# Hybrid encoder layer on one core: router in written order with early indices, first token statistics by pairs, last epsilon on GpSimd

## The chip, the cores and the metric

One core of one Trainium2 chip runs the whole layer in one launch. The metric is the device time of that launch in microseconds (us). Engines are called as in the profile: PE (TensorE matmul), PEld (its weight loads), DVE (VectorE), ACT (ScalarE), POOL (GpSimd), SP (the DMA queue that SyncE issues). Each engine runs its own instructions in the order in which they stand in the program, and waits on semaphores for what others make.

## The reference, cut

```python
# x: (1, 1024, 1024) float32, one layer, h = x at first
n = rms_norm(h, norm1)                    # per token, eps 1e-6
proj = n @ W_in                           # 6656 columns, in blocks
# GDN: 8 heads of 128, both directions, gated delta rule in chunks of 64
# SSD: 16 heads of 64 in 2 groups, both directions, Mamba-2 scan in chunks of 64;
#      decay masks exp(where(incl, cs_i - cs_j, -inf))
h = h + concat(o_gdn, y_ssd) @ W_out
n2 = rms_norm(h, norm2)
aff = softmax(n2 @ W_router)              # 16 experts
vals, idx = top_k(aff.T, 128)             # each expert takes its 128 best tokens
xs = n2[idx]
y = (silu(xs @ W_gate) * (xs @ W_up)) @ W_down * vals
out = rms_norm(h + scatter_add(y, idx), norm_f)
```

## The kernel before, in words

Tokens lie 8 tiles of 128 deep (`x_107` to `x_114`), and 1024 features are 8 blocks `d`. Float32 products are made of rounded parts: an operand is split into a high part (ACT copies it to fp32r: `whi`, or `n`) and the rest (DVE subtracts: `wlo`), and PE multiplies high by high, high by low and low by high. A step of the program is a small function that is put on a list with a slot by `at()` (L134). `flush(name)` (L137) then runs them: for the mixer in the order of a table of 3602 numbers, packed as text in `ORDER["mixer"]`, where a number is the list's index of the step (a step that yields stands several times); for the experts by a heap over the slots.

**Start.** `x_sq(t)` (L344) squares and sums a token tile on ACT, `x_stat(h)` (L347) makes the inverse norm of four tiles at a time (a DVE add-multiply, then the power on POOL through `rsqrt`, L199), `x_scale(t)` (L353) scales a tile on DVE, and `x_turn(h, d)` (L356) transposes four tiles on PE (L359) and evicts them as the two parts `n` (ACT, then DVE). PE turns the small weights `rows` at L334 ahead of that. `w_half` (L250) then does a first projection by halves, L471 turns its result, and `rates` exponentiates a small table of decay rates (`Rf<-Rf 128x48`, on ACT), which it loads from DRAM.

**Mixer.** `w_load`, `w_split` (`whi` on ACT, `wlo` on DVE) and `w_unit` (L242, 6 matmuls) make the projections of 128 columns at a time; convolutions, GDN heads and SSD heads run beside them. For an SSD head, POOL makes a decay mask `E` (a subtraction in L123 and a select, L560), ACT takes its exponential (`E<-E`), DVE goes on. Then the output projection (L1289) adds blocks into `n` with DVE, and `open_moe` (L1445) makes constants on POOL, among them `digit` (L1473, 45 small instructions). All this is inside `tc.manual_schedule()` (L1482): it goes out as it is written.

**Router** (L1485 to 1570). This part is outside of manual scheduling; the tile scheduler places it. Softmax of the logits `lg`; then a search for the 128th largest value of each expert in 15 rounds (L1527 to 1539): DVE compares (`msk`), PE counts with 8 small matmuls (L1533), DVE picks (`best`, a reduction, `trial`). The first expert's weights are split meanwhile: ACT copies the high parts, and DVE makes 12 half rests (`rest()`, `place<-place 128x512`), which are written at one per round from round 2 on. After the search, `ge`, `need`, `sel` and `posx` give every token's place in its expert's list.

**Experts.** `rt(e)` (L1573) makes one-hot tiles `oh` from `posx` (8 DVE instructions), sums them against `aux` on PE (L1580), builds the index `idx` and the gate value on DVE, and issues the gather of 128 token rows (`place<-n2D,idx`, POOL, L1591). `xt` transposes them on PE (L1612) and `gm`, `gs`, `gu`, `ht`, `dm`, `ys` are the expert's products (L1648, L1664, L1667). Expert weights come through SP (`e_load`), 30 of them ahead of the router, each later one when a tile is given back. At the end `TAIL` (L1759) writes out the last norm: `f_sq` (ACT square and sum), `f_st` (L1743: DVE adds epsilon, POOL takes the power), `f_mul` or `f_sc`, `f_out`.

Of the kernel before, what the change touches and what calls it, by code (L numbers as in the profile page):

```python
# [43 lines left out]
        "c-l>v1FU9EvxU35tGlY-v2EM7ZQHhO+qP}nwr$(it@HlLmzyVR)#}x?_nyflXELLdQQ=i2<&;)Y6)CH{3a40wQn3_>;;9%yY!zCCQDIdC6-UKY"  # L44
        "5mjUrP^hA-#G*vviB)_RMN%S_OGQ%&RdSU>6ko_Gq*4ilgerH?Q>Z*Duga%Vs?;h;kQORUkn}=Y*-Ed9sB)6hs&ql}tE56vQ8J;Js-rT<%%BR0"
        "G71GnnN@L>No7$BRJI`5h4MmHRY+A(g;fc;%_LiyRY_G!l~!f`qvHSbGOCiQEM7%b6|W|$rD_NJ>Z*pMnyRzpW~!d5FSD$wE0k58R2T98(IDsz"
        "|2vme6I55#O?6j2R8JKO8cEYwHBr4(Q%TK*R;s1ytNN&Zs<mpPdaG%wtu#|qe>FgSq8g|MsljT93JvX4d(}Zrl8qTcXy~Yhso`pbx-O?O5Dvma"
        "1PB9RVW^5I9tk4DR5enKQlr%vHCaW0v1*)}suDpohz@gAbeO4*L0Pz>W~*6hj*1HDAsu9Z7!Xs)2$>)j#D+K!7iO!uDjsBp_>ce+LKe88ZmFy="
        "UR@P(LJ}wk*HjKsE|{n0tIaAKY*q_ZQb-DkVUe1ywy4CA401zq$OF?=dH5|&3P=fgAs^(20+0$)!(z2W{Zu#AFCjZr5Gui6RSEtn1xwX3wOs8~"
        "D^x*PsVYK6NCRo1FsxFQVYOPL0M@E?YO7kWHmHq4P57g#KoxNf$7LReLQn(@REACJkV3cwyOjk8JJfEqN9|Jw)G64j_N$_BP@RS|a28HLF*pf_"  # L50
        ")nRo+*rtxELHZ<|gF0|r9aAUNNp(t{hYN5KPOIWj0!qReRZ6r=U54$dD%60>@EXpk^YUvstFFOyxB=DSg1V%t!7I1|SK$q86|W9&;T^n(4{%Xk"
        "R#((bxCQs%wh97w)E#wK-BWkqBYc8;sut9Sx=;`93wKq0xUcT32I38&5j=tisuPqJzYAZXF*Jck>XCY=9;>F%3?9Q{Nl&0TJW(y+DYS%E@K8Nb"
        "t)UG(fT!xIdI-<dGx7HDT!ruqy1)zdLcJ0?!b|l!NLxwI;f;DLsU38e^iFk$cd8d`gC5Wm-l{(EUWM=iKB#S?x2iY9(Cy)q>I!|KAH-CjRDb9X"
        "1BBu5Sq&C_R0H9o>I{S6i~1s`4$^giZ|XA)fuS<H!7vyBUm%PQqra=~Y6MJxZ}3%(g3<6py_ED-eTOkH62`(fm?+&3B@Wwx;3tfi?Mad*!F2c~"
        "@;a0brvsY73%_9p{DBz|keiv}Ghmjm19n0<9YN2A+0sVVb6^haf(UxID722KC&Ltoq$BG9MA7qL4@A{b^<Ic3IlBG_O7DaD!c=*BKMdCMVH(U8"
# [53 lines left out]
def trunk(ctx, tc, x, norm1_w, w_in, conv_w, conv_b, gdn_A_log, gdn_dt_bias, gdn_norm_w,  # L109
# [1724 lines left out]
```

## Time and profile before

| | before |
|---|---|
| three timed runs, us | 1672.53, 1676.93, 1685.21 (median 1676.93) |
| the profiled execution, us | 1671.89 |
| its span, us | 1670.2 |
| mean granted PE clock | 0.972 |
| busy us: PE, PEld | 1550.8 (93%), 1264.7 (76%) |
| busy us: DVE, ACT, POOL | 1211.5 (73%), 982.0 (59%), 730.0 (44%) |
| DMA | 254.20 MB, mean 152 GB/s |

Times in rows count from the span's start. Busy time is the time in which an engine ran an instruction; an idle stretch stands in brackets at the instruction that ended it, with what released it. The granted clock is the share of full speed that PE was given: 1.00 is 2.4 GHz and 0.50 is 1.2 GHz.

### The profile page before, as it was taken

What the parts mean: (1) busy time and instruction counts of PE and PEld (TensorE: products, weight loads), DVE (VectorE), ACT (ScalarE), POOL (GpSimd) and SP (SyncE); (2) the same over time, 40 slices, a digit from 0 to 9 for tenths busy, and PEclk for the clock granted to TensorE, in tenths of its full rate; (3) what the DMA queues carried; (4) which work ended last, traced back from release to release, by engine and by line L of the source; (5) the groups of instructions that cost most, each with busy time, mean ns of one, the idle gap of its engine ahead of it and who ended that gap; (6) DMA issues with size and microseconds to landing.
All of it is one profiled execution on the core that took longest, in us unless ns stands there. A gap on an engine that the chain in (4) does not pass through costs nothing. (4 is left out here: it accounts for less than half of the span.)

```text
span 1670.2 us, 23559 instructions
## 1 busy us (share of the span) xinstructions
PE 1550.8 (93%) x8290; PEld 1264.7 (76%) x8290; DVE 1211.5 (73%) x2045; ACT 982.0 (59%) x1788; POOL 730.0 (44%) x533
## 2 busy tenths in 40 slices
PE   5989999999999999998989999998996499899997
PEld 4768888888889888887765687687885377677774
DVE  4686768686767677757779976864556598789875
ACT  5476485858586767465542574243455177677764
POOL 1285263647454654425898877713032011111112
PEclk9999999999999999999999999999997599999999
DMA  4322223223231322222332245457787289999955
GB/s 137 98 60 43 45 65 68 75 56 87 42 98 28 105 70 63 39 70 95 108 101 70 67 135 172 150 183 263 256 284 291 111 311 372 329 382 375 389 184 213
DMA packets 174784, 254.20 MB, mean 152 GB/s; under 512 B 54370, under 2 KB 112027, under 8 KB 174667
## 3 DMA queue, kind: packets, MB, share of 16 engines
q1 hardware_dynamic: 170202, 236.45, 42.3%
q0 software_dynamic: 4464, 16.25, 3.8%
q8 instruction: 65, 1.06, 0.3%
q14 instruction: 53, 0.43, 0.1%
HBM read 221.01 MB, written 31.65 MB: 151 GB/s over the span
## 5 line engine op out<-in xcount | busy, mean ns | idle before, releaser
L242 PE MATMUL pj<-n,whi 128*128 128x512 f32 x1664 | 482.5, 412 | 9.8 <-ACT whi L129 7.5
L242 PEld LDWEIGHTS pj<-n,whi 128*128 128x128 f32 x1664 | 301.0, 190 | 79.2 <-ACT whi L129 11.1
L242 PE MATMUL pj<-n,wlo 128*128 128x512 f32 x832 | 263.4, 398 | 3.6 <-DVE wlo L123 3.5
L123 DVE TENSOR_TENSOR place<-place 128x1024 fp32r<-128x1024 f32 (+1 forms) x182 | 208.0, 1184 | 27.8 <-ACT place L129 27.8
L126 DVE SCALAR_TENSOR_TENSOR cacc<-pj,cols,cacc 128x1023 f32<-128x1023 f32 (+2 forms) x156 | 199.3, 1278 | 22.8 <-POOL cacc L123 20.1
L123 POOL TENSOR_TENSOR cacc<-cacc,cpr 128x1021 f32<-128x1021 f32 x60 | 145.7, 2429 | 153.4 <-ACT cacc L129 81.0
L1648 PE MATMUL pj<-place 128*128 128x512 f32 x768 | 198.3, 410 | 2.0 <-DVE place L123 1.3
L129 ACT ACTIVATE place<-place 128x1024 fp32r<-128x1024 f32 (+1 forms) x181 | 181.5, 1053 | 16.8 <-issue 8.5
L242 PEld LDWEIGHTS pj<-n,wlo 128*128 128x128 f32 x832 | 156.2, 189 | 45.8 <-DVE wlo L123 8.3
L1648 PEld LDWEIGHTS pj<-place 128*128 128x128 f32 x768 | 144.5, 192 | 40.6 <-DVE place L123 5.3
L123 DVE TENSOR_TENSOR n<-n 128x1024 fp32r<-128x1024 f32 x64 | 84.3, 1327 | 68.9 <-ACT n L129 40.7
L1591 POOL DMA_INDIRECT place<-n2D,idx x16 | 17.4, 1088 | 259.4 <-ACT place L129 93.7
L129 ACT ACTIVATE n<-n 128x1024 fp32r<-128x1024 f32 x64 | 66.7, 1056 | 104.1 <-DMA n<-in_w_out_dram 55.2
L123 DVE TENSOR_TENSOR wlo<-wraw,whi 128x512 fp32r<-128x512 f32 x106 | 96.7, 914 | 15.0 <-ACT whi L129 14.9
L1289 PE MATMUL pj<-n 128*128 128x512 f32 x384 | 97.4, 408 | 4.1 <-DVE n L123 4.1
L129 ACT ACTIVATE whi<-wraw 128x512 fp32r<-128x512 f32 x106 | 65.8, 625 | 57.7 <-PE pj L242 47.5
L129 ACT ACTIVATE place<-g 128x512 fp32r<-128x512 f32 (+1 forms) x48 | 26.9, 561 | 110.4 <-PE g L1612 106.2
L1289 PEld LDWEIGHTS pj<-n 128*128 128x128 f32 x384 | 72.5, 191 | 24.2 <-DVE n L123 5.8
L129 ACT ACTIVATE cpr<-pj,cols 128x1021 f32<-128x1021 f32 x60 | 66.5, 1109 | 26.6 <-PE pj L242 16.9
L129 ACT ACTIVATE u<-c,bt 128x128 f32<-128x128 f32 x128 | 39.6, 363 | 60.1 <-DVE ud L123 58.4
L123 POOL TENSOR_TENSOR ex<-N,nm 128x512 f32<-128x512 f32 x48 | 62.2, 1304 | 14.6 <-PE g L785 9.9
L123 DVE TENSOR_TENSOR E<-E,tb_dt 128x1024 f32<-128x1024 f32 x32 | 56.9, 1790 | 15.5 <-ACT E L129 15.3
(328 smaller groups left out, 3202.9 us busy)
## 6 DMA issues: line engine op xcount, KB each, us to landing
place<-in_w_gate_dram SPq DMA_DIRECT2D x64, 512.0 KB, 9.3
place<-in_w_up_dram SPq DMA_DIRECT2D x64, 512.0 KB, 8.7
place<-in_w_down_dram SPq DMA_DIRECT2D x64, 512.0 KB, 9.8
wraw<-in_w_in_dram SPq DMA_DIRECT2D x106, 256.0 KB, 3.3
E<-rowsD SPq DMA_DIRECT2D x32, 512.0 KB, 3.8
n<-mixD SPq DMA_DIRECT2D x64, 256.0 KB, 3.4
n<-in_w_out_dram SPq DMA_DIRECT2D x64, 256.0 KB, 4.4
dec<-rowsD SPq DMA_DIRECT2D x16, 512.0 KB, 7.7
```

What stands on the lines that cost most here:

```text
L123: eng.tensor_tensor(o, a, b, op=op)
L126: V.scalar_tensor_tensor(o, a, s, b, op0=op0, op1=op1, **kw)
L129: S.activation(o, i, f, **kw)
L242: T.matmul(pj[c0][:, hs], lhsT=w[:, d % 4, :], rhs=nn[d][:, hs], start=(d == 0 and a == 0), stop=(d == ND - 1 and a == 2))
L1289: T.matmul(wst["po", r][t], lhsT=m[:, 0, ts], rhs=w[:, 1, :], start=(k == k0 and a == 0), stop=(k == k1 - 1 and a == 2))
L1591: nc.gpsimd.indirect_dma_start(out=ex["xs", e], out_offset=None, in_=n2D[:, :], in_offset=ex["idx", e])
L1648: T.matmul(po, lhsT=xT[:, j, d % 4, :], rhs=wt[k][:, HALF[dd]], start=(d == 0 and a == 0), stop=(d == ND - 1 and a == 2))
```

## The change

Five edits:

1. The statistics of token tiles 0 to 3 are made as soon as two tiles are summed (columns 0:2, then 2:4), and tiles 0 and 1 are scaled ahead of the second pair; tiles 4 to 7 as before.
2. `ORDER["mixer"]` is a new permutation of the same steps (3602 numbers before and after).
3. The router stands inside `tc.manual_schedule()` and so goes out as written; the two casts and two subtractions that fill `aux` move into rounds 0 and 1, and a half rest stands in each of rounds 2 to 13.
4. `rt` no longer gathers; `gx(e)` does. `rt(0)` to `rt(3)` all stand ahead of the first expert, with a yield of 0.5 instead of 6.0, and `gx` stands where the gather stood, 8.7 slots into an expert, from expert 2 on.
5. `f_st` adds epsilon on POOL instead of DVE.

```diff
 ORDER = {
     "mixer":
-        "c-l>v1FU9EvxU35tGlY-v2EM7ZQHhO+qP}nwr$(it@HlLmzyVR)#}x?_nyflXELLdQQ=i2<&;)Y6)CH{3a40wQn3_>;;9%yY!zCCQDIdC6-UKY"
+        "c-lRe1CX@65`}|KI+@S5ZQHhO+qP}nwr$(CZCm&3)L*xrI*rqvytBJCyR$-QVTBjrgc3$L5lX}Y@kD45UW65KL?jVGL=`bWY!OjJ7A&L)BLad%"
...
     def x_sq(t):
         act(junk1, xt[t], AF.Square, accum_out=ss1[:, t:t + 1])
+        if t == 3:
+            scale(0)
+            scale(1)
+        if t in (1, 3):
+            stat(slice(t - 1, t + 1))
+
+    def stat(hs):
+        V.tensor_scalar(ss1[:, hs], ss1[:, hs], 1.0 / D, EPS, op0=OP.mult, op1=OP.add)
+        rsqrt(rstd[:, hs], ss1[:, hs])

     def x_stat(h):
-        hs = slice(h * 4, h * 4 + 4)
-        V.tensor_scalar(ss1[:, hs], ss1[:, hs], 1.0 / D, EPS, op0=OP.mult, op1=OP.add)
         yield 0.1
-        rsqrt(rstd[:, hs], ss1[:, hs])
+        if h:
+            stat(slice(4, NT))

     def x_scale(t):
+        if t > 1:
+            scale(t)
+
+    def scale(t):
         V.tensor_scalar(xt[t], xt[t], rstd[:, t:t + 1], None, op0=OP.mult)
...
-    act(lg, lg, AF.Exp)
-    act(warm, mhalf[:, :1], AF.Silu)
...
+    with tc.manual_schedule():
+        act(lg, lg, AF.Exp)
+        act(warm, mhalf[:, :1], AF.Silu)
...
+        V.memset(best[0][:, 0, :], 0.0)
+        V.tensor_copy(trial, over3(tv["digit"][:, 0, :]))
+        res = hp.tile(SE, F32, name="res")
+        for j in range(15):
+            tt(V, msk3, aff[:, :, None, :].to_broadcast(S4), trialf[:, None].to_broadcast(S4), OP.is_ge)
+            if j < 2:
+                src = res if j else aff
+                V.tensor_copy(aux[:, :, :, 2 + j], src)
+                tt(V, aux[:, :, :, 4] if j else res, src, aux[:, :, :, 2 + j], OP.subtract)
+            elif halves:
+                rest(*halves.popleft())
...
-        yield 6.0
+        yield 0.5 if e < 4 else 6.0
...
-        yield 0.2
+        ex["idx", e], ex["val", e] = bass.IndirectOffsetOnAxis(ap=idx[:, :1], axis=0), ax[:, 6:7]
+
+    def gx(e):
         ex["xs", e] = take()
-        ex["idx", e], ex["val", e] = bass.IndirectOffsetOnAxis(ap=idx[:, :1], axis=0), ax[:, 6:7]
         nc.gpsimd.indirect_dma_start(out=ex["xs", e], out_offset=None, in_=n2D[:, :], in_offset=ex["idx", e])
...
     def f_st(t):
-        V.tensor_scalar(ssf[:, t:t + 1], ssf[:, t:t + 1], D * EPS, None, op0=OP.add)
+        P.tensor_scalar(ssf[:, t:t + 1], ssf[:, t:t + 1], D * EPS, None, op0=OP.add)
...
-    at(-30, rt, 0)
-    at(-29, rt, 1)
+    for e in range(4):
+        at(-30 + 1.9 * e, rt, e)
+        if e < 2:
+            at(-28.8 + 1.9 * e, gx, e)
     for e in range(NE + 1):
         b = EP * e
         if e < NE:
             if e + 2 < NE:
-                at(b + 2, rt, e + 2)
+                if e > 1:
+                    at(b + 2, rt, e + 2)
+                at(b + 8.7, gx, e + 2)
```

Counted over the whole program, ACT has 48 table loads instead of 52, DVE has 7 TENSOR_SCALAR fewer (8 of `f_st` gone, one for the split statistics more), and POOL has 8 TENSOR_SCALAR and one power more; everything else has the same count.

At the start, on ACT, the two orders differ as follows; `n<-g,cols` are the evictions of `x_turn`, `Rf<-Rf 128x48` is the exponential in `rates`, `O<-pj` evicts the result of `w_half`, and + is the new order.

```order
 L129 ACTIVATE n<-g,cols 128x512 x9
+L129 ACTIVATE whi<-wraw 128x512
+L129 ACTIVATE O<-pj 128x1024
+L129 ACTIVATE whi<-wraw 128x512
+L129 ACT_TABLE_LOAD
+L129 ACTIVATE tb_beta<-qd 128x128
+L129 ACT_TABLE_LOAD
+L129 ACTIVATE Rf<-Rf 128x384
+L129 ACTIVATE whi<-wraw 128x512
 L129 ACTIVATE Rf<-Rf 128x48
-L129 ACTIVATE whi<-wraw 128x512
-L129 ACTIVATE n<-g,cols 128x512 x2
```

The exponential `Rf<-Rf 128x48` stood ahead of the last two evictions and now stands behind all of them, behind `O` and behind two table loads.

On DVE, in the output projection of the kernel before, two instructions of the router (L1525 and L1526) stand among the mixer's additions `n`:

```order
L1224 TENSOR_SCALAR Y<-Y,ry 128x512 x8
L123 TENSOR_TENSOR n<-n 128x1024 x8
L1525 MEMSET best_11578 128x16
L1526 COPY trial<-digit 128x48
L123 TENSOR_TENSOR n<-pj,n 128x512 x4
L123 TENSOR_TENSOR n<-n 128x1024 x4
```

In the changed kernel the same two stand on DVE in the router, behind the softmax:

```order
L1502 TENSOR_REDUCE den<-lg 128x8
L1503 RECIPROCAL den<-den 128x8
L123 TENSOR_TENSOR aff<-lg,den 128x128
L1538 MEMSET best_11582 128x16
L1539 COPY trial<-digit 128x48
L123 TENSOR_TENSOR msk_11581<-aff,trial 128x384
L1545 CAST aux<-aff 128x128
```

They moved some 50 rows down, from the output projection to just ahead of the first round.

On ACT, at the first decay masks of the SSD heads, the order before has the weight split `whi` (of the projection block at column 5632) behind two exponentials `E`:

```order
L129 ACTIVATE xk<-g 128x4x128 x2
L129 ACT_TABLE_LOAD
L129 ACTIVATE E<-E 128x1024
L129 ACTIVATE xk<-g 128x4x128
L129 ACTIVATE E<-E 128x1024
L129 ACTIVATE whi<-wraw 128x512
L129 ACTIVATE cacc<-pj,cols 128x1024
```

The changed kernel has it in front of them, with the block's second split behind:

```order
L129 ACTIVATE xk<-g 128x4x128 x3
L129 ACTIVATE whi<-wraw 128x512
L129 ACT_TABLE_LOAD
L129 ACTIVATE E<-E 128x1024 x2
L129 ACTIVATE whi<-wraw 128x512
L129 ACTIVATE cacc<-pj,cols 128x1024
L129 ACTIVATE cpr<-pj,cols 128x1021
```

One `whi` moved from behind the two exponentials to ahead of them.

## Rows read from the trace of the kernel before

**Rows 1.** The page's part 1: busy us, share of span, instructions.
```profile
PE 1550.8 (93%) x8290; PEld 1264.7 (76%) x8290; DVE 1211.5 (73%) x2045; ACT 982.0 (59%) x1788; POOL 730.0 (44%) x533
```

**Rows 2.** Waits of PE: who waits, for whom, us in total, times, longest.
```profile
PE c L1533 <- DVE msk L123: 29.1, 15, 4.3
...
PE pj L242 <- ACT whi L129: 7.5, 2, 4.6
...
PE pj L1289 <- DVE n L123: 4.1, 3, 2.7
```

**Rows 3.** Windows: stretch and length; busy PE, PEld, DVE, ACT, POOL; clock; DMA.
```profile
43.60:50.40 6.80, 5.64 (x18) 4.27 (x18) 2.30 (x6) 3.91 (x5) 0.00 (x0) 0.50 0.13 39
784.30:787.70 3.40, 2.85 (x7) 2.28 (x8) 2.88 (x3) 3.38 (x5) 2.92 (x3) 0.50 0.23 58
...
920.00:940.00 20.00, 19.21 (x71) 12.56 (x70) 19.20 (x22) 7.22 (x8) 19.85 (x12) 1.00 0.22 66
1328.00:1640.00 312.00, 299.55 (x1404) 231.55 (x1402) 261.34 (x403) 217.29 (x266) 44.05 (x29) 0.99 0.89 318
```

**Rows 4.** Timeline of the start: start, us, engine, line, operation, [idle before <-releaser].
```profile
13.89 0.45 PE L334 MATMUL g<-ident,rows 128*128 128x128 f32 x1 [5.02 <-DMA rows<-in_conv_b_dram]
...
33.83 0.69 ACT L129 ACTIVATE n<-g,cols 128x512 fp32r<-128x512 f32 x1 [0.46 <-PE g L359]
...
41.05 0.24 ACT L129 ACTIVATE Rf<-Rf 128x48 f32<-128x48 f32 x1 [6.53 <-DMA Rf<-in_ssd_A_log_dram]
...
41.72 1.25 ACT L129 ACTIVATE n<-g,cols 128x512 fp32r<-128x512 f32 x2
...
42.44 0.50 PE L250 MATMUL pj<-n,whi 128*128 128x512 f32 x1 [3.56 <-ACT n L129]
```

**Rows 5.** Timeline of DVE in the output projection.
```profile
1133.90 0.07 DVE L1525 MEMSET best<- 128x16 f32 x1 [0.49 <-ACT zt L129]
1137.50 0.20 DVE L1526 COPY trial<-digit 128x48 int32<-128x48 int32 x1 [3.52 <-POOL digit L1473]
```

**Rows 6.** Timeline of ACT at the first SSD masks.
```profile
783.22 1.06 ACT L129 ACTIVATE E<-E 128x1024 f32<-128x1024 f32 x1 [2.37 <-POOL E L560]
```

**Rows 7.** Timeline of the router, ACT and DVE.
```profile
1277.22 1.28 ACT L129 ACT_TABLE_LOAD   x1
...
1284.04 0.56 DVE L123 TENSOR_TENSOR msk<-aff,trial 128x384 bf16<-128x384 f32 x1
1284.52 0.68 DVE L123 TENSOR_TENSOR place<-place 128x512 fp32r<-128x512 f32 x1
...
1287.41 0.55 DVE L123 TENSOR_TENSOR msk<-aff,trial 128x384 bf16<-128x384 f32 x1
...
1296.05 0.56 DVE L123 TENSOR_TENSOR msk<-aff,trial 128x384 bf16<-128x384 f32 x1
1297.21 0.21 DVE L126 SCALAR_TENSOR_TENSOR best<-c,trial 128x48 f32<-128x48 f32 x1 [0.60 <-PE c L1533]
...
1297.99 0.56 DVE L123 TENSOR_TENSOR msk<-aff,trial 128x384 bf16<-128x384 f32 x1
```

**Rows 8.** Timeline from `posx` to the first expert, DVE, POOL and PE.
```profile
1316.98 2.69 DVE L1576 TENSOR_SCALAR oh<-slots,posx 128x128 bf16<-128x128 bf16 x16
...
1320.83 1.25 POOL L1591 DMA_INDIRECT place<-n2D,idx  x1 [45.66 <-DVE ax L123]
...
1325.39 1.98 PE L1612 MATMUL g<-ident,place 128*128 128x128 f32 x8 [5.46 <-DMA place<-n2D,idx]
```

**Rows 9.** Timeline of the last norm, POOL and DVE.
```profile
1652.01 1.52 POOL L123 TENSOR_TENSOR rf<-ssf,mhalf 128x1 f32<-128x1 f32 x1 [0.56 <-DVE ssf L1744]
...
1661.13 0.54 POOL L123 TENSOR_TENSOR rf<-ssf,mhalf 128x1 f32<-128x1 f32 x1 [1.46 <-DVE ssf L1744]
...
1662.91 0.20 DVE L1744 TENSOR_SCALAR ssf<-ssf 128x1 f32<-128x1 f32 x2
```

**Rows 10.** Line L1473: ns minimum/median/maximum of one, first and last start.
```profile
L1473 POOL TENSOR_SCALAR digit<-tid x45: 198/208/1232, 1136.9 to 1151.9; 128x1 int32<-128x1 f32 x45
```

More of the change, by code (lines that the diff above doesn't have):

```diff
@@ L1485, in trunk @@
     aff, ones_b, before_b, slots, aux, posx, lg = (tv[n] for n in ("aff", "ones_b", "before_b", "slots", "aux", "posx", "lg"))
-    act(lg, lg, AF.Exp)
-    act(warm, mhalf[:, :1], AF.Silu)
-    den = hp.tile([128, NT], F32, name="den")
-    V.tensor_reduce(den, lg, axis=AX.X, op=OP.add)
-    V.reciprocal(den, den)
-    tt(V, aff, lg, den[:, :, None].to_broadcast(SE), OP.mult)
-    mp = pool("mp")
-    ex = {}
-    halves = deque()
-    def split(w, e, i):
-        raw = eraw.pop(epos[w, e, i])
-        if (w, i) in WHOLE:
-            ex["w", w, e, i] = raw,
-            return None
-        hi, lo = take(F32R), take(F32R)
-        ex["w", w, e, i] = hi, lo
-        act(hi, raw, AF.Copy)
-        return raw, hi, lo
@@ L1507, in rest @@
-    def rest(parts, cols, last):
-        raw, hi, lo = parts
-        tt(V, lo[:, cols], raw[:, cols], hi.bitcast(F32)[:, cols], OP.subtract)
-        if last:
-            give(raw)
-    EARLY = [(w, 0, i) for w in range(2) for i in range(3)]
-    for key in EARLY:
-        parts = split(*key)
-        halves.extend((parts, HALF[h], h) for h in range(2))
-    msk3 = hp.tile([128, NT, 3, NE], BF, name="msk3")
-    best = [hp.tile([128, 4, NE], F32, name=f"best{i}") for i in range(2)]
-    trial = hp.tile([128, 3, NE], I32, name="trial")
@@ L1521, in trunk @@
-    S3 = [128, 3, NE]
-    S4 = [128, NT, 3, NE]
-    trialf = trial.bitcast(F32)
-    over3 = lambda a: a[:, :, None].to_broadcast(S3)
-    V.memset(best[0][:, 0, :], 0.0)
-    V.tensor_copy(trial, over3(tv["digit"][:, 0, :]))
-    for j in range(15):
-        tt(V, msk3, aff[:, :, None, :].to_broadcast(S4), trialf[:, None].to_broadcast(S4), OP.is_ge)
-        if j > 1 and halves:
-            rest(*halves.popleft())
-        pc = ctile([128, 3, NE])
-        for t in range(NT):
-            T.matmul(pc.rearrange("p k e -> p (k e)"), lhsT=ones_b, rhs=msk3[:, t].rearrange("p k e -> p (k e)"),
-                     start=(t == 0), stop=(t == NT - 1))
-        stt(best[j % 2][:, 1:4, :], pc, 127.5, trialf, OP.is_ge, OP.mult)
-        thr = best[1 - j % 2][:, 0, :]
-        V.tensor_reduce(thr, best[j % 2].rearrange("p k e -> p e k"), axis=AX.X, op=OP.max)
-        if j < 14:
-            tt(V, trial, thr.bitcast(I32)[:, None, :].to_broadcast(S3), over3(tv["digit"][:, j + 1, :]), OP.bitwise_xor)
@@ L1553, in trunk @@
-    b_gt, b_eq = pb[:, :NT, :NE], pb[:, :NT, NE:]
-    need = hp.tile([128, 2, NE], F32, name="need")
-    V.tensor_scalar(need[:, 0], pb[:, NT, :NE], -1.0, 128.0, op0=OP.mult, op1=OP.add)
-    V.tensor_scalar(need[:, 1], need[:, 0], 512.0, None, op0=OP.add)
-    needb = lambda i: need[:, i, :][:, None, :].to_broadcast(SE)
-    over = hp.tile(SE, F32, name="over")
-    sel = hp.tile(SE, BF, name="sel")
-    tt(V, over, b_eq, needb(0), OP.subtract)
-    stt(sel, over, 0.0, eq, OP.is_lt, OP.mult)
```

207 lines of the change are left out of this document (126 added, 81 removed).

## The prediction

> **What bounds the kernel now.** I read the page first: PE is busy for 93% of the span and no other engine for more than 76% [rows 1]. So the kernel gets shorter only where PE stands idle or runs at half clock, and I went to PE's waits, ranked, to see whom it waits for [rows 2], and then to the timeline around the long ones. The largest is the router's search, 29.1 us in 15 waits for DVE's compare; two waits of 7.5 us together are for a weight split on ACT (`whi`), and the longest for an addition in the output projection is 2.7 us. The windows show the second price of a wait: the granted clock is at 0.50 (1.2 GHz) in the 6.8 us from 43.6 and in the 3.4 us from 784.3, each right behind an idle PE [rows 3]. Matmul work there runs at half speed, so a stretch costs up to half its length beside the wait: at most 3.4 and 1.7 us.
>
> The expert stage, 1328 to 1640, is 299.6 of 312 us PE [rows 3]. DMA is 0.89 busy there, but a load is issued only when a tile is given back, and tiles are given back by the expert's own progress. I therefore let a gain ahead of the experts move the whole stage; the case against that is a rival below.
>
> **The change, part by part.** All terms are against the profiled execution, 1671.9 us with a span of 1670.2.
>
> *Start (edits 1 and 2).* PE has nothing to do from the last `w_half` matmuls until 42.44, an idle time of 3.56 us that ended with the eviction `n` on ACT. That eviction (two, from 41.72) stood behind the small exponential `Rf`, for which ACT waited 6.53 us until its DMA had landed [rows 4]. The order shows the exponential behind all evictions now, and its consumers later still. Evictions come one per 1.15 us (0.69 of ACT and 0.46 of waiting for PE's next transposes, the row at 33.83). So the last two would start at 33.83 + 1.15 = 34.98 and 36.13 and end near 36.8, in place of 41.72 + 1.25 = 42.97: 6.2 us earlier. The half clock behind that wait, 6.8 us long, costs up to 3.4; the pause before L471 is left and may bring part of it back, so I take 0.9. The pairs let the first tiles be scaled earlier, but the transposes of `x` begin behind the last `rows` turn, which waits for its DMA until 13.89 [rows 4]; its load stands behind as many loads of `x` as before. I give the pairs 0.4. The extra DVE and POOL instruction lie in that wait and cost nothing; without that cover they would cost two short instructions. What is late next is PE's own work: the matmuls of `w_half` behind each eviction. Together **−7.5**; bounds −3 (the eviction pace holds, but heads that are latency chains absorb half) and −10 (the whole half clock is gone and the pairs give 1).
>
> *Output projection (2 and 3).* The tile scheduler had drawn the router's MEMSET and COPY into DVE's mixer stream, where the COPY waited 3.52 us for POOL's `digit` [rows 5]. The additions `n` behind it came late, and PE waited 2.7 us [rows 2]. In the new order the two stand in the router, by when `digit` has been ready for over 100 us (the last starts at 1151.9 [rows 10]). PE then also keeps its clock; as the half clock of the 784 stretch shows, that is up to 1.7 us. I take 2.7 + 1.0 = **−3.7** (0 if the loads of `w_out` are late there anyway, −4.4).
>
> *Router (3).* Three rounds held four half rests each and lasted 3.37 us (1284.04 to 1287.41); a round with none lasts 1.94 (1296.05 to 1297.99). One half takes 0.68 and stands where DVE waits 0.60 for PE's count: from 1284.52 it ends at 1285.20, which is 1.16 after its compare, and without one the next step also starts 1.16 after it (1297.21) [rows 7]. So one half per round is hidden, and 3 × (3.37 − 1.94) = 4.3 us go. The twelve halves now end in round 13, still ahead of the first expert's matmuls. The table load of 1.28 us at 1277.22 stands ahead of the softmax's exponential [rows 7]; a switch to Silu had been put early. It goes behind the exponential. The MEMSET and COPY come onto the path: 0.07 + 0.20 [rows 5]. Together −4.3 − 1.28 + 0.27 = **−5.3** (−4 to −6).
>
> *Early indices (4).* Both `rt` together took 2.69 us of one-hots; alone, the first needs 1.35. Index 0 is thus ready some 1.0 us earlier than at 1320.83, and the gather needs 4.6 us from there to PE's transposes at 1325.39. But now four `rt` stand on DVE ahead of the experts. The small steps of both took 1320.83 − 1319.67 = 1.16, 0.6 each [rows 8], so it is 4 × (1.35 + 0.6) = 7.8 us from 1316.98, and PE's eight matmuls for the fourth index stand ahead of the transposes: 1324.8 plus a part of a microsecond, against 1325.39. I take **0**; bounds −1.0 and +1.0. Gathers on POOL come in the same slots of later experts as before.
>
> *Last norm (5).* `f_st` on DVE queued behind `f_mul` (two of them together at 1662.91, behind a multiply of 1.28 us). On POOL it costs about 0.21 (the median of the small `digit` instructions [rows 10]) and 0.54 for the power [rows 9]. Statistics 6 and 7 would then be ready ahead of their multiplies, and the last multiplies close up: about −1.3. Against that, one power lasted 1.52 instead of 0.54, at 1652.01, with DVE in a multiply of the same kind [rows 9]; if powers stretch so here, one of them puts the last multiply 0.6 back, −0.7. The value is **−0.9**, and +1 is the other bound, when two powers in a row stretch. The Trainium skill (GPSIMD Engine Reference, Key points) says that GpSimd shares its SBUF interfaces with VectorE and contends with DVE instructions that have two SBUF inputs. The trace agrees with 1.52 against 0.54 us; by that rule the term would be −0.7, and by the undisturbed row −1.3.
>
> *Rest of the new table (2).* At the first SSD masks ACT waits 2.37 us for POOL's mask before an `E` exponential [rows 6], and the split `whi` behind it keeps PE waiting. Now this split stands ahead of both exponentials. It is one of the two waits of 7.5 us together, the longer of which is 4.6 [rows 2], so it is 2.9; with half of the 3.4 us at half clock, 4.6. But POOL is as busy as 19.85 of 20 us later in the SSD stage [rows 3], and its work isn't less. Where POOL is the bound, a gain of PE is given back at the next mask. Between −4.6 and 0 I take **−2.3**. The other moved steps I take at 0: their instructions are the same, each moved by some 20 places in 3600.
>
> Sum: −7.5 − 3.7 − 5.3 + 0 − 0.9 − 2.3 = **−19.7**, so 1652.2 in the state of the profiled execution. That one lies 5.0 below the median of the runs, 1676.9, so I forecast **1657 us** for the median; its own range is 1652 to 1663.
>
> **The rivals.**
>
> *Upstream gains are given back.* The start ends earlier, but GDN heads are chains that wait for small instructions of ACT and DVE, and the SSD stage for POOL. For it speaks POOL at 19.85 of 20; against it that PE has so few long waits. With the start at −2 and the table's rest at 0: −2 − 3.7 − 5.3 − 0.9 = −11.9, 1665 us. The expert stage could also return the router's part if its DMA (0.89 busy) doesn't move with the start; −14.4 then, 1662.5.
>
> *The new order also removes the second wait for `whi`.* It is 4.6 and half of a 6.8 us stretch like that at 43.6, 8.0 together. With the first in full: −19.7 − 2.3 − 8.0 = −30, 1647 us. For it: the first such split has moved. Against it: two masks of POOL still stand ahead of the second.
>
> *The other side: new waits for `whi` behind `E`.* The new order puts exponentials back to back and the block's second split behind them. Where POOL is late, each such wait costs up to 8.0. Without the first wait's gain the sum is −17.4, so it decides from three waits on (2.2 × 8.0); slower by over 1% takes 4.3 of them. With five it is −17.4 + 40.0 = +22.6, 1699.5 us. For it: POOL has no slack. Against: only two of these occurred in a mixer of 1260 us.
>
> **How the numbers follow.** My forecast 0.48, gains given back 0.27, second wait removed too 0.15, new waits 0.10. The bound of 1%, about what a measurement of this kernel tells from no change, is at 1660.2 and 1693.7. Four fifths of the forecast's cases lie under 1660.2 (0.39) and all of the third's (0.15): faster 0.54. The rest of the forecast (0.09), the given-back cases (0.27) and new waits that only cancel the gain (0.03) are the same: 0.39. Slower 0.07. The range 1646 to 1673 leaves out the new waits and the lowest part of the third case, some 0.18.
>
> **What would show it.** In the profile after: the evictions at the start without a wait for the rates' DMA, and `w_half` ending near 39; no `digit` wait on DVE; 15 rounds of 1.9 to 2.2 us and no table load ahead of the `lg` exponential; transposes of the first expert as far behind `posx` as before; the tail's powers in sequence on POOL. The prediction is wrong if PE's waits in the SSD stage grow, above all for `whi`, or if the expert stage gets longer than it was.

## The result, and the profile after

The changed kernel takes 1656.83 us (median of 4 runs, 1652.63 to 1659.94) against 1677.95 for the kernel before (4 runs, 1672.53 to 1685.21): 0.987 of it, with a 95% interval of 0.9826 to 0.9914. The forecast was 1657 in a range of 1646 to 1673. The profiled execution took 1656.17 us, with a span of 1654.5 against 1670.2, so the two traces differ by 15.7 us where the sum said 19.7. The account below gives a reason for each.

Part 1 of the page after shows that PE did the same work in a shorter span [rows 1]:

```profile
PE 1550.6 (94%) x8290; PEld 1270.1 (77%) x8290; DVE 1213.4 (73%) x2038; ACT 976.9 (59%) x1784; POOL 731.7 (44%) x542
```

PE's waits after (line numbers are 12 to 18 higher from the middle of the program on) answer [rows 2]:

```profile
PE c L1551 <- DVE msk L123: 23.3, 15, 3.2
...
PE c L1180 <- DVE hs L123: 6.1, 2, 5.3
...
PE pj L1301 <- DVE n L123: 2.4, 3, 1.1
```

The search gave up 5.8 us of waiting, the weight split (7.5 us in two waits) has gone from the list, and the output projection's longest such wait is 1.1 instead of 2.7. But a wait of 5.3 us for `hs`, which was not there before, stands near the top. The windows after show where the clock was at 0.50 (1.2 GHz), and the expert stage:

```profile
40.70:44.10 3.40, 2.75 (x11) 2.56 (x12) 1.18 (x3) 2.80 (x4) 0.00 (x0) 0.50 0.35 97
...
829.20:836.00 6.80, 6.80 (x25) 6.03 (x24) 4.72 (x3) 1.58 (x2) 6.65 (x4) 0.50 0.38 118
866.70:873.50 6.80, 5.52 (x11) 3.50 (x12) 6.32 (x6) 5.81 (x6) 6.73 (x4) 0.50 0.12 35
1314.40:1624.40 310.00, 298.14 (x1388) 231.13 (x1388) 257.93 (x379) 216.27 (x264) 43.47 (x29) 0.98 0.89 321
```

The stretch at the start is half as long as before [rows 3], the one at 784 has moved to 795, and two of 6.8 us stand in the first SSD group, where there was one before (from 876.5).

**Start.** The timeline after, ACT, DVE and PE:

```profile
35.45 1.27 ACT L129 ACTIVATE n<-g,cols 128x512 fp32r<-128x512 f32 x2 [1.15 <-PE g L371]
...
37.04 0.17 DVE L449 TENSOR_REDUCE h<-bd 128x2 f32<-128x8 f32 x1 [1.96 <-POOL bd L403]
...
37.95 1.40 DVE L126 SCALAR_TENSOR_TENSOR n<-g,cols,n 128x512 fp32r<-128x512 f32 x2
...
38.75 0.50 PE L250 MATMUL pj<-n,whi 128*128 128x512 f32 x1 [1.26 <-DVE n L126]
...
41.34 1.97 PE L483 MATMUL g<-ident,O 128*128 128x128 f32 x8 [1.16 <-ACT O L129]
...
49.49 0.23 ACT L129 ACTIVATE Rf<-Rf 128x48 f32<-128x48 f32 x1
```

The last two evictions begin at 35.45 and end at 36.7, as worked out (36.8), and the rates' exponential waits for nothing at 49.49. PE's idle time of 3.56 us [rows 4] is 1.26 now. It isn't zero because a new wait took a part of the place: DVE stood 1.96 us for POOL's block masks (`bd`) ahead of its half of the same evictions.

**Router.** ACT and DVE after:

```profile
1269.49 0.31 ACT L129 ACTIVATE lg<-lg 128x128 f32<-128x128 f32 x1
1269.82 1.28 ACT L129 ACT_TABLE_LOAD   x1
...
1274.72 0.56 DVE L123 TENSOR_TENSOR msk<-aff,trial 128x384 bf16<-128x384 f32 x1
1275.19 0.68 DVE L123 TENSOR_TENSOR place<-place 128x512 fp32r<-128x512 f32 x1
1275.87 0.21 DVE L126 SCALAR_TENSOR_TENSOR best<-c,trial 128x48 f32<-128x48 f32 x1
...
1276.65 0.56 DVE L123 TENSOR_TENSOR msk<-aff,trial 128x384 bf16<-128x384 f32 x1
```

The table load stands behind the exponential, and a round with one half rest lasts 1.93 us, as one without did [rows 7].

**First expert.** DVE, POOL and PE after, to be held against [rows 8]:

```profile
1303.37 1.39 DVE L1589 TENSOR_SCALAR oh<-slots,posx 128x128 bf16<-128x128 bf16 x8
...
1306.30 1.23 POOL L1605 DMA_INDIRECT place<-n2D,idx  x1 [38.47 <-DVE oh L1589]
...
1310.54 1.32 PE L1593 MATMUL c<-aux,oh 128*128 128x5 bf16 x8 [0.89 <-DVE oh L1589]
1311.72 1.95 PE L1626 MATMUL g<-ident,place 128*128 128x128 f32 x8
```

The gather is issued 2.9 us behind the end of `posx` (1303.37) instead of 3.9, and PE turns the gathered rows 8.4 us behind that end, as before: the fourth index's matmuls stand in between and PE waits for nothing else.

**Last norm.** POOL and DVE after, [rows 9]:

```profile
1637.24 1.28 DVE L126 SCALAR_TENSOR_TENSOR place<-place,rf 128x1024 f32<-128x1024 f32 x1 [1.04 <-POOL rf L123]
1637.43 1.18 POOL L1758 TENSOR_SCALAR ssf<-ssf 128x1 f32<-128x1 f32 x1 [0.22 <-ACT place L129]
...
1639.24 0.23 POOL L1758 TENSOR_SCALAR ssf<-ssf 128x1 f32<-128x1 f32 x1
1639.30 1.28 DVE L126 SCALAR_TENSOR_TENSOR place<-pj,rf,place 128x1024 f32<-128x1024 f32 x1 [0.77 <-POOL rf L123]
1639.55 0.57 POOL L123 TENSOR_TENSOR rf<-ssf,mhalf 128x1 f32<-128x1 f32 x1
...
1640.40 0.57 POOL L123 TENSOR_TENSOR rf<-ssf,mhalf 128x1 f32<-128x1 f32 x1
...
1649.09 1.28 DVE L126 SCALAR_TENSOR_TENSOR place<-pj,rf,place 128x1024 f32<-128x1024 f32 x1
```

The epsilon takes 0.22 to 0.25 us on POOL (0.21 had been taken), and twice 1.16 to 1.18, each time beside a multiply of DVE such as the one at 1637.24, which takes both its tensors from SBUF (`place<-place`). Beside the multiply at 1639.30, which takes one from PSUM (`pj`), the power takes 0.57 as elsewhere.

**First SSD group.** The chain to the wait of 5.3 us after, ACT, DVE and PE:

```profile
862.91 1.06 ACT L129 ACTIVATE E<-E 128x1024 f32<-128x1024 f32 x1 [3.01 <-POOL E L572]
...
864.52 0.78 DVE L123 TENSOR_TENSOR wlo<-wraw,whi 128x512 fp32r<-128x512 f32 x1 [2.59 <-ACT whi L129]
865.22 2.11 DVE L123 TENSOR_TENSOR E<-E,tb_dt 128x1024 f32<-128x1024 f32 x1
867.25 0.68 DVE L123 TENSOR_TENSOR hs<-c,hs 128x512 f32<-128x512 f32 x1
...
867.98 2.07 PE L1180 MATMUL c<-xw,Bt 128*128 128x512 f32 x2 [5.30 <-DVE hs L123]
```

ACT waited 3.0 us for POOL's mask, the split behind it came late, DVE waited for the split, and `hs`, for which PE waits, stood behind both. PE waits for another name than in the kernel before; at the end of the chain is the same POOL mask.

### The profile page after: what moved, and what is told of

Same layout as the page of the kernel before. It is cut to its first block, busy times and chain, and to the rows that moved or that the text cites. A ratio compares the mean times of both kernels' runs of the same rounds, so it can differ in the third digit from the quotient of the medians.

```text
span 1654.5 us, 23564 instructions
## 1 busy us (share of the span) xinstructions
PE 1550.6 (94%) x8290; PEld 1270.1 (77%) x8290; DVE 1213.4 (73%) x2038; ACT 976.9 (59%) x1784; POOL 731.7 (44%) x542
## 3 DMA queue, kind: packets, MB, share of 16 engines
q8 instruction: 65, 1.06, 0.3%
## 5 line engine op out<-in xcount | busy, mean ns | idle before, releaser
L242 PE MATMUL pj<-n,whi 128*128 128x512 f32 x1664 | 484.7, 413 | 3.0 <-DVE cacc L126 1.3
L242 PEld LDWEIGHTS pj<-n,whi 128*128 128x128 f32 x1664 | 302.1, 191 | 71.6 <-issue 7.3
L242 PE MATMUL pj<-n,wlo 128*128 128x512 f32 x832 | 263.1, 397 | 0.6 <-DVE wlo L123 0.6
L242 PEld LDWEIGHTS pj<-n,wlo 128*128 128x128 f32 x832 | 157.1, 189 | 40.2 <-DVE wlo L123 1.9
L123 DVE TENSOR_TENSOR wlo<-wraw,whi 128x512 fp32r<-128x512 f32 x106 | 101.8, 964 | 26.4 <-ACT whi L129 26.3
L123 POOL TENSOR_TENSOR E<-E,tb_gc 128x1024 f32<-128x1024 f32 x32 | 65.6, 2048 | 9.7 <-DMA E<-rowsD 4.9
## 6 DMA issues: line engine op xcount, KB each, us to landing
place<-in_w_up_dram SPq DMA_DIRECT2D x64, 512.0 KB, 10.7
```

The lines of the kernel that those rows point to most:

```text
L123: eng.tensor_tensor(o, a, b, op=op)
L242: T.matmul(pj[c0][:, hs], lhsT=w[:, d % 4, :], rhs=nn[d][:, hs], start=(d == 0 and a == 0), stop=(d == ND - 1 and a == 2))
```

## The experiments

Every column of this table is one profiled execution; the rows are starts in us, read from the timelines. Blocks are the projection's column blocks of 48 matmuls each, counted from 0 in the order in which PE runs them (block 0 is that of `w_half`, L250, the others are L242). Product 456 is the 456th matmul `pj<-place`. The two tables give PE different orders, so from one table to the other the start of a single block in the SSD stage is no measure of a gain: the last column begins the output projection within 0.4 us of the changed kernel and is 11.5 us ahead of it at block 44.

| start of | before | after | router alone | table alone | rates alone | old table, all else |
|---|---|---|---|---|---|---|
| scalar transposes (L471) | 46.9 | 41.3 | 46.9 | 41.8 | 43.3 | 43.6 |
| block 20 | 413.0 | 408.1 | 418.1 | 408.4 | 409.9 | 407.6 |
| block 39 | 784.8 | 775.1 | 788.9 | 774.9 | 781.2 | 777.7 |
| block 44 | 865.0 | 869.7 | 869.3 | 867.9 | 861.7 | 858.2 |
| output projection (L1289) | 1042.3 | 1035.6 | 1046.7 | 1032.9 | 1039.4 | 1035.3 |
| last step of `lg` | 1277.0 | 1269.2 | 1277.2 | 1268.5 | 1275.5 | 1269.3 |
| first compare | 1279.7 | 1270.8 | 1279.4 | 1271.3 | 1278.2 | 1270.9 |
| last compare | 1311.5 | 1297.9 | 1306.5 | 1303.0 | 1310.0 | 1298.0 |
| first product of the experts | 1327.2 | 1313.6 | 1322.2 | 1318.9 | 1325.8 | 1313.4 |
| product 456 of the experts | 1467.5 | 1451.6 | 1461.7 | 1457.8 | 1466.0 | 1451.5 |
| last multiply | 1664.9 | 1649.1 | 1661.8 | 1657.9 | 1666.0 | 1647.4 |

**The router alone** (edit 3 in the kernel before).

```diff
-    act(lg, lg, AF.Exp)
+    with tc.manual_schedule():
+        act(lg, lg, AF.Exp)
...
```

> The kernel before with edit 3 alone (router inside manual scheduling, with its written order). If the terms of the prediction add up, the search lasts 27.1 us from its first to its last compare instead of 31.8, the table load is gone from the path, the output projection loses its 2.7 us wait and the half clock behind it, and the whole is 9 us shorter (-5.3 -3.7). The rival is that the output projection is held by its weight loads: then the stall goes but the stream waits a little later, the logits come 1.5 us earlier at most, and the whole is 7 us shorter.

Measured: 0.9917 (0.989 to 0.9943), 1666.64 us. From the first compare to the last it is 27.1 us, as expected; the first compare comes 2.2 us behind `lg` instead of 2.7. Its waits in the output projection show that the stall there is gone:

```profile
PE pj L1289 <- DVE n L123: 2.8, 3, 1.4
```

From the begin of the output projection to `lg` it lasts 230.5 us against 234.7. Windows of the last 150 us of that stretch, first of the kernel before and then of this run, show what PE did in it:

```profile
1122.30:1277.00 154.70, 147.25 (x729) 123.19 (x728) 72.97 (x89) 75.30 (x104) 40.86 (x87) 0.97 0.76 260
```

```profile
1126.80:1277.20 150.40, 144.40 (x729) 120.77 (x728) 72.16 (x88) 73.15 (x102) 43.19 (x87) 1.00 0.78 264
```

PE stands idle for 7.5 us before and for 6.0 here. So of the 2.7 us of the stall 1.5 are gained with the router alone. The rest of the 4.2 us goes with the half clock: 8.0 us of this stretch ran at it before, and 0.6 here. By the medians the whole is 11.1 us shorter and by the ratio 13.9 (9.6 to 18.5), more than the better of the two expectations (9).

This run also showed how single executions differ. Up to the output projection its instructions are those of the kernel before, and yet block 20 comes 5.1 us later. Windows and PE's timeline of this run, and then of the kernel before, around the place:

```profile
290.00:300.00 10.00, 10.00 (x40) 9.03 (x39) 6.67 (x10) 5.59 (x15) 6.27 (x4) 0.51 0.58 171
...
287.61 1.59 PE L755 MATMUL g<-cm,ex 128*128 128x16 f32 x13 [0.51 <-DVE cm L126]
```

```profile
290.00:300.00 10.00, 10.00 (x67) 8.91 (x66) 9.58 (x12) 8.25 (x18) 8.11 (x5) 1.00 0.79 236
...
287.00 1.26 PE L755 MATMUL g<-cm,ex 128*128 128x16 f32 x10 [0.24 <-DVE cm L126]
```

PE was idle for 0.51 us here in the one and for 0.24 in the other. Behind it the clock was at its lower level for 10 us in the one, 40 matmuls instead of 67, and at full speed in the other. The idle time at this place alone doesn't decide that: in the run with one split moved (below) PE is idle for 0.54 us here, and the clock is at 1.00 from 290 to 300 us.

**The new table alone** (edit 2 in the kernel before; the diff is the table).

> The kernel before with edit 2 alone (the new table). If the table's gain is that of the start, the second projection block begins 5.5 us earlier and the whole is 6 to 7 us shorter. If the new table also helps or hurts in the masks of the SSD heads by more than 2 us, the shift at the begin of the output projection is not 5 to 7 us. The router's MEMSET and COPY may still be drawn into the mixer, so the stall in the output projection may stay.

Measured: 0.9956 (0.9935 to 0.9976), 7.4 us. The block behind the start (block 1) begins 5.9 us earlier, as expected (5.5), and PE's longest wait for `n` in the output projection is still 1.6 us. The output projection begins 9.4 us earlier in the profiled execution, of which 5.9 were there at block 37 (743.06 against 748.95). The two columns with the new table differ by 2.7 us at the output projection, though nothing ahead of it differs between them but the pairs. So the shift in SSD isn't told from chance by these two. Router alone and table alone multiply to 0.9917 × 0.9956 = 0.9873, the whole change. That would leave nothing for edits 1, 4 and 5, but the two intervals have room for some 5 us.

**One step of the old table** (two of its entries: the rates' exponential and the negation behind it).

```diff
-            for i in np.frombuffer(zlib.decompress(base64.b85decode(ORDER[name])), "<u2").tolist():
+            seq = np.frombuffer(zlib.decompress(base64.b85decode(ORDER[name])), "<u2").tolist()
+            seq.insert(141, seq.pop(106))
+            seq.insert(141, seq.pop(106))
+            for i in seq:
```

> The kernel before with one step of its own table moved: the small exponential of the decay rates and the negation behind it come after the scalar projection's first steps instead of ahead of the last two evictions. My step says that this alone is the start's gain: the first projection's transposes begin 6 to 7 us earlier, and the whole is 6 to 7 us shorter. The rival says that the heads are chains that do not start earlier by the full amount: 5.5 us earlier there, 3 us or less at the end.

Measured: 0.9956 (0.9936 to 0.9976), 7.4 us, the same as the whole new table. The shift at the transposes is 3.5 us, where 6 to 7 had been expected, and at block 5 (98.0 against 103.1) 5.1; in this execution 3.4 of it are left at block 37, behind one more stretch of 3.4 us at half clock (from 284.1). Within these intervals (3.4 us to either side) the one moved step carries what the new table is worth, and the rival's 3 us or less lies outside of its own (4.0 to 10.7).

**Everything but the new table**: the table of before, with that one step moved, in the changed kernel (first lines of the two tables).

```diff
 ORDER = {
     "mixer":
-        "c-lRe1CX@65`}|KI+@S5ZQHhO+qP}nwr$(CZCm&3)L*xrI*rqvytBJCyR$-QVTBjrgc3$L5lX}Y@kD45UW65KL?jVGL=`bWY!OjJ7A&L)BLad%"
...
+        "c-l>v1FU9EvxU35tGlY-v2EM7ZQHhO+qP}nwr$(it@HlLmzyVR)#}x?_nyflXELLdQQ=i2<&;)Y6)CH{3a40wQn3_>;;9%yY!zCCQDIdC6-UKY"
...
...
+            seq.insert(141, seq.pop(106))
+            seq.insert(141, seq.pop(106))
...
```

> All of the change but the new table: the kernel before's own table with the one step of the decay rates moved, and edits 1, 3, 4 and 5. If the start's gain is that one step, and the rest of the new table gives as much as it takes, this is as fast as the changed kernel (21 us below the kernel before). If the new table's rest is worth something, it is 3 us or more slower than the changed kernel.

Measured: 0.9887 (0.9849 to 0.9926), 1658.48 us, against 0.987 of the changed kernel: the same within their intervals (some 6 us to either side). The rest of the permutation, 3600 places, has no measurable worth.

**The split ahead of the exponential**, alone.

```diff
...
+            seq.insert(2359, seq.pop(2370))
...
```

> The kernel before with one step of its own table moved: the weight split of column block 5632 comes ahead of the first decay mask's exponential. The prediction took -2.3 us, between -4.6 (the wait of 2.9 us for the split and half of 3.4 us at half clock are gone for good) and 0 (PE gets ahead, waits for a later mask of GpSimd, and all is given back by 870 us into the run). The changed kernel's trace speaks for 0: there the block behind it came 9.7 us earlier and the one at 870 us 4.7 us later.

Measured: 1.0001 (0.9984 to 1.0018). PE at this place before, and then ACT, DVE and PE of this run:

```profile
784.85 2.07 PE L242 MATMUL pj<-n,whi 128*128 128x512 f32 x4 [2.89 <-ACT whi L129]
```

```profile
780.80 0.63 ACT L129 ACTIVATE whi<-wraw 128x512 fp32r<-128x512 f32 x1 [6.65 <-DMA wraw<-in_w_in_dram]
...
783.83 1.33 DVE L123 TENSOR_TENSOR E<-E,tb_dt 128x1024 f32<-128x1024 f32 x1 [2.84 <-ACT E L129]
785.08 1.27 DVE L126 SCALAR_TENSOR_TENSOR cacc<-pj,cols,cacc 128x1021 f32<-128x1021 f32 x1
...
786.50 2.05 PE L244 MATMUL pj<-n,whi 128*128 128x512 f32 x4 [2.67 <-DVE cacc L126]
```

The split is ready at 781.4, and PE still waits, 2.67 us instead of 2.89. It needs the accumulator `pj` of an earlier block, and the convolution tap that frees it (`cacc`) stands on DVE behind a multiply that waits for the same exponential.

**The tap moved too.**

```diff
...
+            seq.insert(2359, seq.pop(2370))
+            seq.insert(2363, seq.pop(2364))
...
```

> The kernel before with two steps of its own table moved: the split of block 5632 ahead of the first mask's exponential, as in the run before, and on VectorE the convolution's last tap ahead of the multiply that waits for that exponential. If two waits lay at one place (the split, and under it the buffer that the tap gives free), PE's idle time of 2.7 us near 783 is gone now, with the half clock behind it, and block 40 comes 4 us earlier. Whether it lasts: if GpSimd is the bound behind it, less than 1 us of it is left by block 46 (near 922 us); if not, 4 us.

Measured, one run: 1683.68 us, with several long stretches at half clock. DVE and PE of this run:

```profile
787.57 1.54 DVE L123 TENSOR_TENSOR E<-E,tb_dt 128x1024 f32<-128x1024 f32 x1 [1.36 <-ACT E L129]
789.03 2.39 DVE L123 TENSOR_TENSOR wlo<-wraw,whi 128x512 fp32r<-128x512 f32 x1
...
791.47 0.80 PE L245 MATMUL pj<-n,wlo 128*128 128x512 f32 x1 [2.82 <-DVE wlo L123]
```

PE takes its four high products and then waits 2.82 us for the low part, which stands behind the same multiply. Three waits lay on top of each other, all fed by one late exponential. So "block 40 comes 4 us earlier" was wrong as well. Against the kernel before, this run is 5.8 us late at block 37, 2.7 at block 39 and 7.2 at block 40, where it stays: the 3.1 us by which block 39 began earlier were lost within that block, in the wait for `wlo` and a stretch of 6.8 us at half clock behind it (3.4 before).

**Less work for POOL in the first SSD group's masks**, in both kernels.

```diff
     def dec_mask(dd, row, di):
-        tt(P, dd, dd, tb["gc"][:, :, row:row + 1].to_broadcast(C8), OP.subtract)
+        m = 1 if row >= 16 and row % 16 < 8 else NT
+        tt(P, dd[:, :m], dd[:, :m], tb["gc"][:, :m, row:row + 1].to_broadcast([128, m, 128]), OP.subtract)
```

> The changed kernel, but GpSimd subtracts the row of only one of eight chunks in each decay mask of the first SSD group (so these masks are wrong, and the output with them): some 1.7 us less on GpSimd in each of 16 masks. If GpSimd's masks hold PE in the first SSD group, PE's waits of 5.3, 2.1 and 2.0 us there are gone, and the output projection begins 8 us or more earlier than in the changed kernel. If they are waits of VectorE's own making, it begins less than 3 us earlier.

> The kernel before with the same work left out (the subtraction of seven of eight chunks in the first group's decay masks). If the two tables only place the waits for GpSimd differently, both lose their long waits for it, and the changed kernel's lead at the output projection stays what it was at the last GDN head (6 us); if the new table was made worse by GpSimd alone, its lead grows by 4 us or more.

Measured, one run each: 1644.73 us (after) and 1665.04 (before). The output projection begins at 1023.7 us (after; 1035.6 with the work in) and at 1031.2 (before; 1042.3): 11.9 and 11.1 us earlier. Windows of 140 us over the group, first of the changed kernel and then of the kernel before, each without the work:

```profile
770.00:910.00 140.00, 131.78 (x598) 98.77 (x596) 107.58 (x101) 65.80 (x73) 98.64 (x70) 0.99 0.30 96
```

```profile
785.00:925.00 140.00, 131.32 (x595) 96.58 (x595) 109.40 (x105) 60.00 (x69) 109.39 (x73) 1.00 0.29 93
```

POOL is busy for 99 and 109 us of 140 here, against 118 and 125 in the same windows with the work in, and the clock is at 0.99 and 1.00, against 0.94 and 0.97. So a part of the gain is the half clock behind the waits: half of its length in this group is 8.5 us with the work and 1.7 without in the changed kernel, and 5.1 and 0 in the kernel before, an estimate of 6.8 and 5.1 us of the 11.9 and 11.1. Of the changed kernel's waits of 5.3, 2.1 and 2.0 us, one of 2.5 (`hs`) and one of 1.5 (`E`) are left. The lead of the changed kernel is 7.5 us at the output projection, against 5.7 at block 37 (742.6 and 748.3) and 6.6 in the profiled pair with the work in. By these four executions both orders lose about the same to POOL's masks; they only put the waits at other places. Of the two expectations for each kernel the first held, but for the two waits that are left.

**Early indices: two instead of four.**

```diff
-    for e in range(4):
+    for e in range(2):
...
-        if e < 2:
-            at(-28.8 + 1.9 * e, gx, e)
+        at(-28.8 + 1.9 * e, gx, e)
...
-                if e > 1:
-                    at(b + 2, rt, e + 2)
+                at(b + 2, rt, e + 2)
```

> The changed kernel with indices 2 and 3 back behind the first expert's begin; the gathers stand where the change has them. The prediction took 0 for early indices because the fourth index ends later than the first gather lands. If so, the first expert's transposes now begin 7.4 us after posx instead of 8.7 (the gather's landing decides), some 1.0 us or more earlier, and the first experts lose part of it again to VectorE's one-hots. If the gather lands late for a reason of its own, the 8.7 us stay.

Measured, one run: 1665.81 us. PE of this run:

```profile
1314.50 1.36 PE L1593 MATMUL c<-aux,oh 128*128 128x5 bf16 x8 [0.88 <-DVE oh L1589]
1319.46 1.98 PE L1626 MATMUL g<-ident,place 128*128 128x128 f32 x8 [3.60 <-DMA place<-n2D,idx]
```

The transposes come 7.8 us behind the start of the last step of `posx` (1311.66) instead of 8.7 (from 1303.05): 0.9 earlier, with the gather's landing as what ended last. But product 456 of the experts comes 141.2 us behind the first one, against 138.0 with four early indices. By these two executions, DVE's one-hots between the experts cost 3.2 us, more than the start gains.

**The pairs undone**, in the changed kernel.

```diff
-        if t == 3:
-            scale(0)
-            scale(1)
-        if t in (1, 3):
-            stat(slice(t - 1, t + 1))
...
+    def x_stat(h):
+        hs = slice(h * 4, h * 4 + 4)
         V.tensor_scalar(ss1[:, hs], ss1[:, hs], 1.0 / D, EPS, op0=OP.mult, op1=OP.add)
+        yield 0.1
         rsqrt(rstd[:, hs], ss1[:, hs])
...
-        if h:
-            stat(slice(4, NT))
...
-        if t > 1:
-            scale(t)
...
```

> The changed kernel with edit 1 undone: statistics of four tiles at a time. The prediction gave the pairs 0.4 us, because the transposes of x wait for the small weights' DMA. The changed kernel's trace says less: if those weights decide, the transposes of the scalar projection begin within 0.3 us of 41.3; if the pairs carry the start, they begin 1 us or more later.

Measured, one run: 1661.85 us. The scalar projection's transposes begin at 42.1 us against 41.3. The run with two early indices has the pairs, and there they begin at 42.4. So runs of the same code ahead of this place lie up to 1.1 us apart, and what the pairs give is within that.

**ScalarE takes the subtraction.** If POOL costs 11 us there, another engine might do this work, with nothing left out:

```diff
...
         def e_exp(hh, di):
-            act(st["E", hh, di], st["E", hh, di], AF.Exp)
+            dd = st["E", hh, di]
+            if g:
+                act(dd, dd, AF.Exp)
+                return
+            k = di * 8 + hh
+            for c in range(NT):
+                act(dd[:, c], dd[:, c], AF.Exp, bias=tb["nege"][:, c, k:k + 1])
```

> The changed kernel, faster if GpSimd holds the first SSD group: the subtraction of the 16 first masks is taken from GpSimd and made by ScalarE as the bias of the exponential (8 instructions of 128x128 in place of one of 128x1024, with a table of negated columns made once). Nothing is left out. If GpSimd is the bound, as leaving the work out showed (12 us), and ScalarE, busy for 55 of 140 us there, takes it up, the whole is 8 us or more faster than the changed kernel. If ScalarE's longer exponentials keep the weight splits behind them waiting, less than 3 us is gained or something is lost.

Measured: 0.9927 (0.9906 to 0.9948), 1665.82 us, against 0.987 (0.9826 to 0.9914) and 1656.83 us of the changed kernel: some 9 us slower, with intervals that just touch. ACT and PE of this run:

```profile
784.16 2.45 ACT L129 ACTIVATE E<-E,tb_nege 128x128 f32<-128x128 f32 x8
...
790.00 0.66 PE L1071 MATMUL g<-ident,BT 128*128 128x128 f32 x4 [2.69 <-ACT xk L129]
```

An exponential takes 2.45 us in eight parts instead of 1.06, and the evictions behind it (`xk`) now keep PE waiting, for 2.69 us at this place. So something is lost, as the second expectation had it, though the evictions at this place are others than the weight splits that it named; that all of the loss comes from there is not shown.

**One direction of it, in the old table** (the kernel that has everything but the new table).

```diff
...
-            dec_mask(st["E", hh, di], 16 + di * 16 + g * 8 + hh, di)
+            dec_mask(st["E", hh, di], 16 + di * 16 + g * 8 + hh, di, g > 0 or di == 0)
...
+            if g or di == 0:
+                act(dd, dd, AF.Exp)
+                return
...
```

> The kernel with the old table and all other edits (as in the run of that name), and the subtraction moved from GpSimd to ScalarE's bias for only one direction of the first group, 8 masks of 16. If what spoiled the version with 16 masks was ScalarE's longer exponentials at places where GpSimd was not late, half of them in the table that has fewer such waits gains 3 to 5 us against the old table's 1658 us. If every microsecond taken from GpSimd comes back on ScalarE, it is as fast or slower.

Measured: 0.9867 (0.9851 to 0.9884), 1656.3 us against 1658.48 for the old table without it and 1656.83 for the changed kernel. The three can't be told apart. No version was found that beats the changed kernel by a measurable amount.

## Why the prediction was right, and where it was not

The median fell by 21.1 us and the forecast said 20 (1677 to 1657), so the size and the sign are right. That 1656.83 lies 0.2 us from the forecast is luck, for two errors of 4 us cancel. The sum, −19.7, was made against the profiled execution of 1671.9 us, which lies at the low end: in the runs taken beside the experiments, 25 of the kernel before reach from 1671.15 to 1682.24 with a median of 1677.72. The changed kernel's profiled execution, 1656.17, is close to its own median of 1656.83. So the sum was 4.0 us too large between the two traces (−15.7), and the 5.0 us added for the median were 4.3 too many for the changed kernel. What makes an execution long or short, the runs showed above: stretches at half clock that come or stay away in identical code. From the start to the end of the experts, without the long one of the router, the clock is at half for 30.7 us in the trace before and for 37.5 in the one after; half of the difference, an estimate of 3.4 us, is most of the 4.0.

By its steps:

- *Start, −7.5.* The step is right and its size somewhat large: 5.5 us at the transposes, 5.9 at block 5, 5.7 at block 37. ACT's evictions ended where they were forecast (36.7). Missed was DVE's wait of 1.96 us for POOL's block masks, queued ahead of the last two. The half clock behind it shrank from 6.8 to 3.4 us. That the moved exponential is the main cause is shown by moving it alone: it gives 3.5 of the 5.5 us at the transposes and 5.1 of the 5.9 at block 5.
- *The pairs, 0.4.* Within 1.1 us of nothing, as the DMA-bound start suggested.
- *Output projection, −3.7.* This is the term whose size was furthest off. The stall went (the longest wait is 1.4 us with the router alone and 1.1 in the changed kernel, instead of 2.7), and so did the 3.4 us at half clock behind it (from 1139.3): such a stretch, once of 6.8 us, stands there in all five traces with a stall of 2.6 or 2.7 us and in none of the three of the same table without it. But the wait's length was taken for its price, and PE's idle time in the whole stretch, 7.5 us before, is 6.0 with the router alone and 7.4 in the changed kernel. What is left at the logits is 1.1 us in the changed kernel (234.7 to 233.6 from its begin), 4.2 with the router alone and 0.7 with the old table. The half clock of the router begins 3.1, 0.6 and 8.9 us ahead of the logits in these three, and 4.6 before; with half of each length taken off, an estimate, they gain 0.4, 2.2 and 2.9. Why the half clock begins where it does stays open.
- *Router, −5.3.* 5.8: 1.1 from the softmax and 4.7 from the rounds. The best founded term, made of rows alone, and the most exact.
- *Early indices, 0.* Right for the first transposes (0.1), by the mechanism named: the run with two indices shows both the 0.9 us that the gather would have given and that the fourth index takes it. Missed was what they do later: between the first product and product 456 it is 138.0 us now, and 137.8 to 138.4 in all six traces with four early indices, against 138.9 to 142.1 in the seven with the old schedule (the two longest have one more stretch of 3.4 us at half clock), so some 1 to 2 us were gained where DVE has no one-hots to make. I had weighed only the way to the first expert.
- *Last norm, −0.9.* 1.4: the last multiply begins 17.7 us behind the first addition of the tail (1631.41 to 1649.09), against 19.1 before (1645.81 to 1664.90; the stretch behind is in [rows 9]); it is 17.7 in all seven traces with this edit and 19.1 in all seven without it. The contention with VectorE that the prediction weighed is there, but it hit the cheap instruction, the epsilon (1.18 instead of 0.22), and the powers took 0.57 throughout; before, one power took 1.52. The price was paid once in each half of the tail, where it had little behind it.
- *Rest of the table, −2.3.* This is the step whose mechanism failed. "It is one of the two waits of 7.5 us together, the longer of which is 4.6 [rows 2], so it is 2.9" took the name of a wait for its whole cause. Two more waits lay under it, for `cacc` and for `wlo`, and one moved split was worth nothing (1.0001). The bound of 0 came out, though not by the path that it names (a gain "given back at the next mask"): with the split alone nothing was gained that could be given back. The end of the chain is the one that the prediction named, POOL's mask, for which the exponential waits. What the new table as a whole gives from block 37 to the output projection is little: 292.3 us in the changed kernel against 293.3, and 289.8 to 293.8 in three further traces with the new table, 293.4 to 294.1 in three with the old. The reading of blocks 39 and 44 in the split's expectation (9.7 us ahead, then 4.7 behind) says less than it seems to, since the changed kernel is 8.2 us ahead again at block 46: PE's order is another one there.
- *The expert stage moves as a whole.* Right: 13.6 us at the first product, 15.9 at product 456 and to near the end. Some 1.5 us came back behind that, with a stretch of 3.4 us at half clock from 1624.5.

Of the rivals, "upstream gains are given back" was right in a part only: the start's gain stayed, but the table's rest gave little. Both waits for `whi` (7.5 us) did go, as the second rival had it, and new waits behind `E` did come, as the third had it (5.3 us for `hs`); the one made up for the other, and neither moved the sum.

## What to carry to other kernels

A wait named in a profile is only the one that came last: before a move is priced by its length, ask what else the waiting engine needed at that moment and whether that is fed by the same late instruction. Terms built from rows of one dependent chain (the router's rounds) came out within 10%; a reordering in a stage whose side engine is nearly full can be worth nothing (1.0001 here). And a sum made against one profiled execution inherits its luck: ask first where that execution lies among the runs.

## What the runs showed that was not expected

The same instruction stream ran 5.1 us apart at block 20 in the router-alone run and 7.3 in the run with split and tap moved, ahead of any difference to the kernel before. In the first, one stretch of 10.2 us at 1.2 GHz makes the difference; the second has the same one and a longer one at the start (10.2 instead of 6.8 us). PE's idle time just ahead was 0.51 and 0.39 us in these two and 0.24 in the kernel before, but 0.54 in the split-alone run, which kept full speed there. So what decides it stays open, and a difference of 5 us between two single executions isn't evidence for a change.

Work taken off a nearly full engine doesn't come free on one with room: seven eighths of 16 subtractions left out were worth 11 to 12 us at the output projection (one execution each), and all 16 moved to ScalarE, which was busy for 60 to 66 of 140 us in the windows above, cost about 9 us against the changed kernel.
